# Gate products stacked into one fp32r product, and norm rows from two, in a decoder trunk

## The chip, the cores and the metric

One Trainium2 chip (trn2), of which the kernel uses one core. The metric is the device time of the kernel in microseconds. The kernel before ran three times: 2303.4, 2303.47 and 2307.49 us, median 2303.47. Profiles show one further execution of each kernel.

The engines are called as in the profile: PE (TensorE, matmuls; PEld is its weight load), DVE (VectorE), ACT (ScalarE), POOL (GpSimd) and SP (SyncE, which issues nearly all transfers).

## What is computed

A decoder trunk on 256 tokens of width 2048, two layers, in float32. Layer 0 mixes by gated linear attention (GLA, 4 heads), layer 1 by forgetting attention (FoX, 12 heads); each layer also attends to 256 memory tokens and ends in a gated MLP with a causal convolution of width 3. Cut to what the change touches:

```python
def rmsnorm(x, g):
    y = x * rsqrt(mean(x * x, axis=-1) + EPS)
    return y * g

# GLA: z = h @ w_in is split into q, k, v, glr, og, mq; glr is 16 wide
g = log_sigmoid(glr @ w_gate_up + b_gate) / 16        # forget gates, 4 heads x 256
o = gla_chunked(q, k, v, g)                           # 4 heads, o is 384 wide in each
o = o * rsqrt(mean(o * o, axis=-1) + EPS) * gn_gain   # a norm of each head's output
```

## The kernel before

The activations stay on the chip, features on the 128 partitions and the 256 tokens along the free dimension. The weights are streamed once, in units of up to 128x1024 floats: SP loads `raw` (L190), ACT rounds it to fp32r as `whi` (L191), and DVE subtracts (`wlo` = raw - whi, L200). Activations are split in the same way, high half and low half side by side in one tile of 2 x 256 columns. A float32 product is made of three fp32r products, high by high, low by high and high by low.

- `proj_fm` gives features on partitions. For each block of 128 rows, `product` (L222 to L228) issues `whi` against both halves at once (512 columns, L225 or L228) and `wlo` against the high half (256 columns, L226). `whole` (L233, L235) adds the two halves of the result.
- `proj_tm` gives tokens on partitions, with three products of up to 512 columns (L262 to L264).

Everything small is done in plain fp32: transposes by an identity, attention scores, and the two things that this case is about.

**Gates.** The first value panel also gives the 16 columns of `glr`, scaled by the norm's column. `turned` (L268 to L282) copies them to a zeroed tile (`narrow`, L274), transposes it (L279), and L491 copies the result to `glr`, 16 features on partitions 0 to 15 and zeros below. For each head `gates` loads 128x256 of `w_gate_up`, zero below row 16 (L510, two buffers), and for each of two halves multiplies it with `glr` (L514: fp32, 128x128 weights, 256 columns). ACT (L517 to L519) and DVE (L521 to L523) make the running sums of the log gates from it. The sums feed `core`, a head's attention by levels: subtractions (L578), exponentials (L579) and products (L581) on DVE and ACT, many small fp32 matmuls on PE (L595), masked copies back (L607).

**Norm rows.** A norm has a column `y`, one number for each token on its partition, found by Newton steps on DVE (L324 to L327), and a row, the same numbers along the free dimension on every partition, by which results with features on partitions are multiplied. `Norm.row` makes it once for each norm: DVE multiplies the identity by `y` for each half of the tokens (`dg`, L346), PE multiplies a matrix of ones by that diagonal (L348: fp32, 256 columns), and ACT copies the sum to `row` (L351). There are nine rows: memory, layer 0 input, four GLA heads, the two MLPs, and one for FoX.

**What sets the order.** The program is written in the order of the layers, and a scheduler places each engine's instructions when the kernel is built; each engine then takes its own in that order and waits on semaphores. Weight units are asked for 300 places ahead (`tc.high_priority`), with four buffers for `raw` and three each for `whi` and `wlo`. A heavier or lighter instruction can therefore move others on all engines.

Of the kernel before, what the change touches and what calls it, by code (L numbers as in the profile page):

```python
# [12 lines left out]
F32 = mybir.dt.float32  # L13
F32R = mybir.dt.float32r
I32 = mybir.dt.int32
AF = mybir.ActivationFunctionType
ALU = mybir.AluOpType
PSUM = bass.MemoryType.PSUM

P = 128  # L20
T = 256
# [4 lines left out]
GLA_H, DK, DV = 4, 256, 384  # L26
FOX_H, HD = 12, 128
MEM_H = 4
RANK = 16
# [108 lines left out]
def _trunk(ctx: ExitStack, tc: tile.TileContext, xt, xtok, memt, wp, wgu, gns, gfin, cnv, par, msk, out):  # L138
    nc = tc.nc
    where, _ = _layout()  # L140
    V, S, TE = nc.vector, nc.scalar, nc.tensor

    const = ctx.enter_context(tc.tile_pool(name="const", bufs=1))
    wpool = ctx.enter_context(tc.tile_pool(name="wpool", bufs=4))
    sm = ctx.enter_context(tc.tile_pool(name="small", bufs=2))
# [9 lines left out]
    ident = mask[:, M_ID : M_ID + P]  # L155
    ones = mask[:, M_ONE : M_ONE + P]
# [3 lines left out]
    def gain(name, i):  # L160
        c = C_GAIN[name] + i
        return gains[:, c : c + 1]

    eps = const.tile([P, 1], F32, name="eps")
    nc.gpsimd.memset(eps, EPS)
# [11 lines left out]
    def work(tag, bufs=1):  # L177
        return pwork.tile([P, 512], F32, name="ps_" + tag, tag=tag, bufs=bufs)
# [86 lines left out]
                if u == len(units) - 1:  # L265
                    evac(b, a)

    def turned(pool, bank, width, col):  # L268

        t = pool.tile([P, T], F32, name="narrow", tag="tmp", bufs=5)  # L270
        nc.gpsimd.memset(t, 0.0)

        def take(b, a):
            S.activation(t[:, b * P : b * P + width], a, AF.Copy, scale=col[:, b : b + 1])  # L274

        def turn():
            for b in range(2):
                bs = slice(b * P, (b + 1) * P)
                TE.transpose(bank[:, bs], t[:, bs], ident)  # L279
            return bank[:, :T]  # L280

        return take, turn  # L282
# [11 lines left out]
    class Norm:  # L294
# [45 lines left out]
        def row(self):  # L340

            if self.r is None:
                y = self.col()
                dg = sm.tile([P, T], F32, name="dg", tag="sq", bufs=2)
                for b in range(2):
                    V.tensor_scalar(dg[:, b * P : (b + 1) * P], ident, y[:, b : b + 1], None, ALU.mult)  # L346
                pr = work("t")
                TE.matmul(pr[:, :T], ones, dg, start=True, stop=True)  # L348
                self.r = sm.tile([P, T], F32, name="row", tag="rowx" if self.tag == "x" else "row",
                                 bufs=2 if self.tag == "x" else 1)  # L350
                S.activation(self.r, pr[:, :T], AF.Copy)  # L351
            return self.r
# [51 lines left out]
    nx = StreamNorm()  # L404
    with tc.tile_pool(name="load", bufs=1) as lp:
        mt = [lp.tile([P, 4, T], F32, name=f"mt{i}") for i in range(4)]

        def take_mem(g, half):
            n = 2 if g == 0 else 4
            if n == 2 or half == 0:  # L410
                i = half * 2
                nc.sync.dma_start(mt[g][:, i : i + n, :], memt[g, :, i : i + n, :])
                for i in range(i, i + n):
                    split(bufA, 4 * g + i, mt[g][:, i, :], gain("mem", 4 * g + i))
# [41 lines left out]
        for i in range(KC):  # L456
            split(bufB, i, xf[i], gain("mix0", i))
# [12 lines left out]
    def gla(nx):  # L470
        h, mix = bufB, bufA
        with tc.tile_pool(name="gla", bufs=1) as gp:
# [3 lines left out]
                nc.gpsimd.memset(t, 0.0)  # L476
            on = {}

            glr = gp.tile([P, T], F32, name="glr")

            def values(hd):
                return gp.tile([P, 2, DV], F32, name="gv", tag="gv", bufs=2)

            v0 = values(0)
            take, turn = turned(gp, work("t"), RANK, nx.col())

            def first_values(b, a):
                S.activation(v0[:, b, :], a[:, :DV], AF.Copy, scale=nx.col()[:, b : b + 1])
# [17 lines left out]
            def gates(hd):  # L506

                bc = gp.tile([P, 2, T], F32, name="bc", tag="bc", bufs=2)
                wg = gp.tile([P, DK], F32, name="wg", tag="wg", bufs=2)
                nc.sync.dma_start(wg, wgu[hd])  # L510
                for c in range(2):
                    f = 2 * hd + c
                    ps = work("s", 2)
                    TE.matmul(ps[:, :T], wg[:, c * P : (c + 1) * P], glr, start=True, stop=True)  # L514
                    bias = part[:, C_BG + f : C_BG + f + 1]
                    e = gp.tile([P, T], F32, name="ge", tag="tmp", bufs=5)
                    S.activation(e, ps[:, :T], AF.Abs, bias=bias)  # L517
                    S.activation(e, e, AF.Exp, scale=-1.0)
                    S.activation(e, e, AF.Ln, bias=1.0)  # L519
                    mz = gp.tile([P, T], F32, name="gm", tag="tmp", bufs=5)  # L520
                    V.tensor_scalar(mz, ps[:, :T], bias, 0.0, ALU.add, ALU.min)  # L521
                    V.tensor_tensor(mz, mz, e, ALU.subtract)
                    V.tensor_tensor_scan(bc[:, c, :], scanmask, mz, 0.0, ALU.mult, ALU.add)  # L523
                return bc
# [111 lines left out]
            for hd in range(GLA_H):  # L636
                bc = gates(hd)
                q = gp.tile([P, 2, T], F32, name="gq", tag="gq", bufs=2)
                k = gp.tile([P, 2, T], F32, name="gk", tag="gk", bufs=2)
                v = values(hd) if hd else v0  # L640
                proj_fm(("gq", hd), h, lambda c, a: V.scalar_tensor_tensor(
                    q[:, c, :], whole(a), DK ** -0.5, nx.row(), ALU.mult, ALU.mult))
                proj_fm(("gk", hd), h, lambda c, a: V.tensor_tensor(k[:, c, :], whole(a), nx.row(), ALU.mult))
                if hd == GLA_H - 1:
                    for j in range(OG_EARLY):
                        take_og(j)
                if hd:
                    proj_tm(("gv", hd), h, lambda b, a: S.activation(
                        v[:, b, :], a, AF.Copy, scale=nx.col()[:, b : b + 1]))
                core(hd, q, k, v, bc)  # L650
# [4 lines left out]
    def fox(nx, vt):  # L655
        hk, hq, mix = bufB, bufA, bufB
        stash = vt.rearrange("p b (i t) -> p (b i) t", t=T)
        with (
# [5 lines left out]
            for j in range(6):  # L664
                proj_fm(("fk", j), hk, lambda c, a, j=j: V.tensor_tensor(kt[:, 2 * j + c, :], whole(a), nx.row(), ALU.mult))
                for i in range(2 * j, 2 * j + 2):
                    split(hq, i, stash[:, i, :], gain("mix1", i))
            cs = fp.tile([P, T], F32, name="fc")
            cc = fp.tile([P, 2, FOX_H], F32, name="fcc")
            take, turn = turned(fp, work("s", 2), FOX_H, nx.col())  # L670

            def forget():
# [120 lines left out]
    def preparing(name, dst, also=None):  # L793
# [18 lines left out]
        return n, then  # L812

    gla(nx)
    n, then = preparing("ffn0", bufB)
    add_out(("wo", 0), bufA, then)
# [18 lines left out]
    with tc.tile_pool(name="store", bufs=1) as op:  # L835
        gf = op.tile([P, D], F32, name="gf")
        nc.sync.dma_start(gf, gfin.to_broadcast([P, D]))
        y = op.tile([P, 2, 512], F32, name="y")
# [93 lines left out]
```

## Time and profile before

| | |
|---|---|
| median of three runs | 2303.47 us |
| the profiled execution, its own time | 2304.12 us |
| its span, first to last instruction | 2302.3 us |
| granted PE clock, mean | 0.999 |
| PE matmul, busy | 2284.6 us |
| DVE, busy | 1614.8 us |
| ACT, busy | 1253.2 us |
| L348 (nine rows), matmul records | 18, 5.3 us busy |
| L514 (eight gate products), matmul records | 16, 5.1 us busy |
| GLA heads | 115 to 392 us of the span |

How to read it: the span is one execution, so it stands beside its own time and not beside the median. A matmul's duration holds its passage through the array, of which the next one covers a part; what it costs in a stream is the distance from its start to the next start. An engine's busy time says little of what it costs the kernel if another engine is the one that everything waits for; that is seen in the chain of work that ended last and in what ended an engine's idle time.

### The profile page before, as it was taken

How to read it: one execution, taken by the hardware profiler on the slowest of the kernel's cores; microseconds unless marked ns; L12 is line 12 of the kernel's file. 1: busy time of each engine (PE TensorE's matmuls, PEld its weight loads, DVE VectorE, ACT ScalarE, POOL GpSimd, SP SyncE). 2: the span in 40 equal slices, each digit the busy share in tenths (PEclk: the TensorE clock that was granted, in tenths of full speed). 3: DMA queues.
4: the chain of work that ended last, by engine and by line, in shares of the span. 5: the costliest groups of instructions: out<-in, count | busy, mean ns of one | idle time of the engine just before them, and what ended most of it. 6: DMA issues, size and time to landing. Idle time of an engine off the chain costs nothing.

```text
span 2302.3 us, 33124 instructions
## 1 busy us (share of the span) xinstructions
PE 2284.6 (99%) x12384; PEld 1976.7 (86%) x12384; DVE 1614.8 (70%) x2635; ACT 1253.2 (54%) x1958; POOL 3.0 (0%) x19
## 2 busy tenths in 40 slices
PE   8999999999999999999999999999999999999998
PEld 7889988888888888888888998888888888888886
DVE  7568987577765777557767557657776577756775
ACT  6555565555553555445565455556554455534554
POOL 0000000000000000000000000000000000000000
PEclk9999999999999999999999999999999999999999
DMA  8655555555555555555555564555555655565554
GB/s 309 200 160 158 156 158 179 188 183 190 187 191 193 191 188 188 192 192 191 186 184 189 176 195 157 167 190 187 189 191 191 193 185 190 189 195 190 186 191 156
DMA packets 124745, 430.14 MB, mean 187 GB/s; under 512 B 14108, under 2 KB 18600, under 8 KB 124456
## 3 DMA queue, kind: packets, MB, share of 16 engines
q1 hardware_dynamic: 124296, 427.50, 57.6%
q8 instruction: 97, 1.59, 0.3%
q14 instruction: 64, 0.52, 0.1%
q10 hardware_dynamic: 288, 0.52, 0.1%
HBM read 425.86 MB, written 2.11 MB: 186 GB/s over the span
## 4 chain that ended last, share of the span: by engine, by line
PE 99%; DMA 0%; ACT 0%; DVE 0%; issue 0%; SPq 0%; DVEq 0%; ACTq 0%
PE acc L225 37%; PE acc L226 20%; PE acc L263 12%; PE acc L264 12%; PE acc L262 12%; PE acc L228 2%; PE ps_s L806 0%; PE ps_s L595 0%; PE ps_t L380 0%; PE ps_s L387 0%; PE ps_o L398 0%; DMA mt<-memt 0%; PE ps_s L720 0%; PE ps_o L614 0%; PE ps_o L736 0%; PE ps_s L514 0%
## 5 line engine op out<-in xcount | busy, mean ns | idle before, releaser
L200 DVE TENSOR_TENSOR wlo<-raw,whi 128x1024 fp32r<-128x1024 f32 (+4 forms) x809 | 972.5, 1203 | 543.8 <-ACT whi L191 531.1
L191 ACT ACTIVATE whi<-raw 128x1024 fp32r<-128x1024 f32 (+4 forms) x809 | 843.2, 1043 | 772.0 <-PE acc L264 370.2
L225 PE MATMUL acc<-B,whi 128*128 128x512 f32 x1980 | 684.1, 396 | 0.0
L225 PE MATMUL acc<-A,whi 128*128 128x512 f32 x1680 | 580.7, 397 | 7.2 <-ACT whi L191 7.2
L226 PE MATMUL acc<-B,wlo 128*128 128x256 f32 x2112 | 551.1, 281 | 0.0
L226 PE MATMUL acc<-A,wlo 128*128 128x256 f32 x1792 | 464.6, 281 | 0.5 <-DVE wlo L200 0.5
L225 PEld LDWEIGHTS acc<-B,whi 128*128 128x128 f32 x1980 | 360.9, 188 | 69.0
L226 PEld LDWEIGHTS acc<-B,wlo 128*128 128x128 f32 x2112 | 397.6, 188 | 21.7
L225 PEld LDWEIGHTS acc<-A,whi 128*128 128x128 f32 x1680 | 305.8, 188 | 63.9 <-ACT whi L191 7.6
L226 PEld LDWEIGHTS acc<-A,wlo 128*128 128x128 f32 x1792 | 338.1, 189 | 21.1 <-DVE wlo L200 1.4
L263 PE MATMUL acc<-wlo,B 128*128 128x512 f32 (+3 forms) x736 | 274.9, 374 | 1.3 <-DVE wlo L200 1.3
L264 PE MATMUL acc<-whi,B 128*128 128x512 f32 (+3 forms) x736 | 274.0, 373 | 0.0
L262 PE MATMUL acc<-whi,B 128*128 128x512 f32 (+3 forms) x736 | 247.6, 372 | 0.0
L263 PE MATMUL acc<-wlo,A 128*128 128x512 f32 x544 | 212.4, 390 | 0.0
L264 PE MATMUL acc<-whi,A 128*128 128x512 f32 x544 | 211.8, 389 | 0.0
L262 PE MATMUL acc<-whi,A 128*128 128x512 f32 x544 | 192.9, 391 | 0.0
L233 ACT ACTIVATE part<-acc 128x256 f32<-128x256 f32 x240 | 90.1, 376 | 163.1 <-PE acc L228 163.1
L263 PEld LDWEIGHTS acc<-wlo,B 128*128 128x128 f32 x736 | 138.2, 188 | 21.1 <-DVE wlo L200 1.7
L264 PEld LDWEIGHTS acc<-whi,B 128*128 128x128 f32 x736 | 138.3, 188 | 18.7
L262 PEld LDWEIGHTS acc<-whi,B 128*128 128x128 f32 x736 | 137.5, 188 | 18.7
L235 DVE TENSOR_TENSOR wholes<-acc,part 128x256 f32<-128x256 f32 x240 | 101.1, 421 | 66.3 <-ACT part L233 65.9
L264 PEld LDWEIGHTS acc<-whi,A 128*128 128x128 f32 x544 | 102.1, 188 | 21.2
(196 smaller groups left out, 1565.6 us busy)
## 6 DMA issues: line engine op xcount, KB each, us to landing
raw<-wp SPq DMA_DIRECT2D x743, 512.0 KB, 3.4
raw<-wp SPq DMA_DIRECT2D x32, 384.0 KB, 3.1
raw<-wp SPq DMA_DIRECT2D x24, 388.0 KB, 3.1
raw<-wp SPq DMA_DIRECT2D x8, 400.0 KB, 3.2
xf<-xt SPq DMA_DIRECT2D x16, 128.0 KB, 4.8
x<-xtok SPq DMA_DIRECT2D x4, 512.0 KB, 7.2
mt<-memt SPq DMA_DIRECT2D x3, 512.0 KB, 7.7
cb<-cdram SPq DMA_DIRECT2D x12, 128.0 KB, 3.4
```

The costliest lines, as they stand in the source:

```text
L191: casts.append(S.activation(hi[:, s], raw[:, s], AF.Copy))
L200: V.tensor_tensor(lo[:, s], raw[:, s], hi[:, s].bitcast(F32), ALU.subtract)
L225: TE.matmul(a, hi[:, s], both, start=done == 0, stop=False)
L226: TE.matmul(a[:, :T], lo[:, s], both[:, 0, :], start=False, stop=False)
L228: TE.matmul(a, hi[:, s], both, start=False, stop=True)
L233: S.activation(t, a[:, T:], AF.Copy)
L235: V.tensor_tensor(r, a[:, :T], t, ALU.add)
L262: TE.matmul(a, xk[:, 0, xs], hi[:, s], start=u == 0 and j == 0, stop=False)
L263: TE.matmul(a, xk[:, 0, xs], lo[:, s], start=False, stop=False)
L264: TE.matmul(a, xk[:, 1, xs], hi[:, s], start=False, stop=last)
```

## The change

Gates: the copies of `glr` are written three times, at rows 0, 32 and 64 of the transposed tile: the value rounded to fp32r twice, and the remainder. The weights lie at the same three places (in the host's array). They are cast to fp32r on ACT, and rows 32 to 63 are replaced by the remainder on DVE. One fp32r product of 128 rows then sums high by high, high by low and low by high. `raw` weights and `wg` have one buffer each.

Norm rows: the column is split into a rounded part and a remainder, each gets its diagonal (one instruction with both halves of the tokens), and two fp32r products with an fp32r matrix of ones sum them. That matrix is a new constant. The split of activations and weights into two halves, and all other fp32 products, stay as they are.

```diff
+    onesr = const.tile([P, P], F32R, name="onesr")
+    nc.gpsimd.memset(onesr.bitcast(F32), 1.0)
...
-    def turned(pool, bank, width, col):
+    def turned(pool, bank, width, col, parts=False):
...
         def take(b, a):
-            S.activation(t[:, b * P : b * P + width], a, AF.Copy, scale=col[:, b : b + 1])
+            o = [t[:, b * P + i : b * P + i + width] for i in (0, 32, 64)]
+            if not parts:
+                S.activation(o[0], a, AF.Copy, scale=col[:, b : b + 1])
+                return
+            for i in range(2):
+                S.activation(o[i].bitcast(F32R), a, AF.Copy, scale=col[:, b : b + 1])
+            V.scalar_tensor_tensor(o[2], a, col[:, b : b + 1], o[0], ALU.mult, ALU.subtract)
...
                 y = self.col()
-                dg = sm.tile([P, T], F32, name="dg", tag="sq", bufs=2)
-                for b in range(2):
-                    V.tensor_scalar(dg[:, b * P : (b + 1) * P], ident, y[:, b : b + 1], None, ALU.mult)
+                y2 = [sm.tile([P, 2, 1], F32R, name=f"y{i}", tag=f"y{i}") for i in range(2)]
+                V.tensor_copy(y2[0], y.unsqueeze(2))
+                V.tensor_tensor(y2[1], y.unsqueeze(2), y2[0].bitcast(F32), ALU.subtract)
                 pr = work("t")
-                TE.matmul(pr[:, :T], ones, dg, start=True, stop=True)
+                for i, yi in enumerate(y2):
+                    dg = sm.tile([P, 2, P], F32R, name="dg", tag="sq", bufs=2)
+                    V.tensor_tensor(dg, ident.unsqueeze(1).to_broadcast([P, 2, P]),
+                                    yi.bitcast(F32).to_broadcast([P, 2, P]), ALU.mult)
+                    TE.matmul(pr[:, :T], onesr, dg, start=i == 0, stop=i == 1)
...
-            glr = gp.tile([P, T], F32, name="glr")
+            glr = gp.tile([P, T], F32R, name="glr")
...
-            take, turn = turned(gp, work("t"), RANK, nx.col())
+            take, turn = turned(gp, work("t"), RANK, nx.col(), True)
...
-                wg = gp.tile([P, DK], F32, name="wg", tag="wg", bufs=2)
-                nc.sync.dma_start(wg, wgu[hd])
+                raw = gp.tile([P, DK], F32, name="wgraw", tag="wgraw")
+                nc.sync.dma_start(raw, wgu[hd])
+                wg = gp.tile([P, DK], F32R, name="wg", tag="wg")
+                S.activation(wg, raw, AF.Copy)
+                V.tensor_tensor(wg[32:64], raw[32:64], wg[32:64].bitcast(F32), ALU.subtract)
...
-    wgu[:RANK] = a["gla_w_gate_up"][0]
+    for i in (0, 32, 64):
+        wgu[i : i + RANK] = a["gla_w_gate_up"][0]
```

## The prediction

> **What bounds the kernel now.** I read the page first: the busy shares, the slices, the chain that ended last.
>
> ```profile
> span 2302.3 us, 33124 instructions
> ## 1 busy us (share of the span) xinstructions
> PE 2284.6 (99%) x12384; PEld 1976.7 (86%) x12384; DVE 1614.8 (70%) x2635; ACT 1253.2 (54%) x1958; POOL 3.0 (0%) x19
> ...
> DVE  7568987577765777557767557657776577756775
> ...
> PEclk9999999999999999999999999999999999999999
> ...
> PE 99%; DMA 0%; ACT 0%; DVE 0%; issue 0%; SPq 0%; DVEq 0%; ACTq 0%
> ```
>
> PE is busy for 2284.6 of 2302.3 us at full granted clock, and the chain is PE for 99%. So time is PE's work plus its few waits. The waits view of PE alone lists 7.2 us for L225 (the first loads, before 12.7 us), 1.3 us for L263 and 0.5 us for L226; nothing else. A nanosecond taken from any matmul is a nanosecond of span, while VectorE (DVE) and ScalarE (ACT) work is free as long as they stay ahead of PE. DVE is nearest to the bound in slices 4 and 5 (230 to 345 us, the GLA heads), with digits 9 and 8.
>
> A busy PE is modelled, so what a matmul costs has to be read from starts. The timeline of PE, around a norm row (L348) and around a gate product (L514), columns start, duration:
>
> ```profile
> 51.84 0.39 PE L262 MATMUL acc<-whi,A 128*128 128x512 f32 x1
> 52.07 0.59 PE L348 MATMUL ps_t<-dg,mask 128*128 128x256 f32 x2
> 52.31 0.58 PE L262 MATMUL acc<-whi,A 128*128 128x512 f32 x1
> 52.73 0.39 PE L263 MATMUL acc<-wlo,A 128*128 128x512 f32 x1
> ...
> 162.17 0.60 PE L514 MATMUL ps_s<-glr,wg 128*128 128x256 f32 x2
> 162.41 0.47 PE L226 MATMUL acc<-B,wlo 128*128 128x256 f32 x1
> 162.72 0.39 PE L225 MATMUL acc<-B,whi 128*128 128x512 f32 x1
> 162.95 0.28 PE L226 MATMUL acc<-B,wlo 128*128 128x256 f32 x1
> 163.07 0.39 PE L225 MATMUL acc<-B,whi 128*128 128x512 f32 x1
> ```
>
> One fp32 product leaves two records (x2). An fp32r product of 512 columns takes 0.23 us from start to start (51.84 to 52.07), one of 256 columns 0.12 (162.95 to 163.07). From L348's start to the matmul after its successor are 52.73 - 52.07 = 0.66 us; less the successor's 0.23, **an fp32 product of 256 columns costs 0.43 us**. The gate gives the same: 162.72 - 162.17 = 0.55, less 0.12. The other places of both lines give 0.426 to 0.438. Where two L226 follow each other the spacing is 0.112 to 0.119, median 0.117.
>
> **The change, part by part.**
>
> *Gates.* Eight fp32 products (4 heads x 2) become eight fp32r ones of the same 256 columns: 8 x (0.432 - 0.117) = **-2.52 us**. The nearest row is L226, same shape and type; its bounds give -2.46 to -2.61.
>
> *Norm rows.* Nine fp32 products (18 records of L348) become eighteen fp32r ones: 9 x (0.432 - 2 x 0.117) = **-1.78 us**, by the bounds -1.7 to -1.9. I count no more: the built program has 9 more PE instructions, and otherwise the same ones in another order.
>
> The Trainium skill, page "TensorE: Matmul & The Clock Gate", section "Back-to-back issue gap", puts the isolated gap at N/2.4 + 2.5 ns, an estimate of 109 ns for 256 columns; by it the sum would be 8 x 0.323 + 9 x 0.214 = 4.5 us instead of 4.3. The trace shows 0.112 at the least, so I keep the row.
>
> *DVE.* Each row replaces two multiplications by two wider ones and gains two tiny ones; each head gains a subtraction. The rows:
>
> ```profile
> L346 DVE TENSOR_SCALAR dg<-mask,ny 128x128 f32<-128x128 f32 x18 | 4.3, 282 | 0.2
> L378 DVE TENSOR_SCALAR p<-p,rc 128x256 f32<-128x256 f32 x16 | 5.5, 352 | 0.5
> L522 DVE TENSOR_TENSOR gm<-gm,ge 128x256 f32<-128x256 f32 x8 | 3.3, 416 | 0.0
> L324 DVE TENSOR_TENSOR nt<-ny 128x2 f32<-128x2 f32 x27 | 4.2, 157 | 0.5
> ```
>
> The new diagonal has no row; L378 (0.35) and L522 (0.42) bound it, and L522 is the same operation, so 0.42. A row costs 2 x 0.42 + 2 x 0.16 - 2 x 0.28 = +0.6 us, nine of them 5.4. The weight subtractions add 4 x 0.42 = 1.7 and the low gate part 2 x 0.3: 7.7 us in all. The skill's page "VectorE: DVE Perf Modes", section "The perf-mode tier table", speaks against this trade: fp32 tensor_scalar in SBUF runs at 2x, tensor_tensor at 1x. L378 against L522 agrees (0.35, 0.42).
>
> I cost this at nothing, for two reasons. DVE has 687 us of idle time, and it runs ahead of PE: the first row's diagonal ends at 47.38 (lines L346 and L348 taken singly) and its product starts at 52.07; seven of nine have 3.5 us or more, the others 2.9 and 1.35 (at 238 us). 0.6 us fits into each. Without that cover, the heads' share is at risk: 4 rows x 0.6, 3 subtractions, 0.6 for the low part, 4.3 us.
>
> *ACT, SP, POOL.* Four casts of 128x256 (L518: 0.41) and two more narrow copies (L274: 0.26) come to 2.2 us of ACT, idle for 46% of the span. The added wait is at the first cast: ACT stands until its wgu load lands (issued at 38.95, 3.8 us: 42.75), with the next weight casts queued behind it and PE behind those. There ACT idles 1.66 us before the cast at 43.88 anyway, so it hides. Casts of later heads wait for the gate weights' single buffer; in the built order each stands right behind the Abs of the head before, which already waited for that product. The wgu loads, now single-buffered, stay within a few places of SP's queue; the load before has long been read. The POOL memset of 128x128 (0.2 us or so, by L476: 0.42 for 384) is needed at 52 us. The last matmul ends 8.7 us before the end; that tail isn't touched.
>
> **Sum.** -2.52 - 1.78 = -4.30 us. The profiled execution took 2304.12 us (span 2302.3 and 1.8 around it), so 2299.8 by its own time; it lies 0.65 us above the median of the runs, 2303.47, from which the sum is 2299.2. I say **2299.5 us**, 0.17% under the median. What a measurement of this kernel can tell from no change is about 0.2%, 4.6 us; the sum stops 0.3 us short of that line.
>
> **The rivals.**
>
> *Faster by more than the line.* The one PE wait in mid-kernel, 1.34 us at 1315.9, ends a chain that has nothing to do with PE's pace: ACT's table load at L677 (1.28 us), then the forget sums through memory (cdram, cb), and DVE standing at L715 for cb while the next wlo waits behind it. If the new order or the earlier PE moves it apart, 2303.5 - 4.3 - 1.3 = 2297.9. Against it: in the built order DVE and SP stand there as before. Shorter spacing (0.112) alone gives 2299.0. But 0.3 us is little beside runs that lie 4 us apart (2303.4 to 2307.49), so part of the forecast's own chance falls beyond the line.
>
> *DVE's cover is gone in the heads.*
>
> ```profile
> core 0: us, PE busy (x) PEld busy (x) DVE busy (x) ACT busy (x) POOL busy (x), PEclk, DMA share, GB/s
> 230.00:320.00 90.00, 90.00 (x601) 80.24 (x601) 83.56 (x212) 52.75 (x92) 0.00 (x0) 1.00 0.49 151
> ```
>
> Only 6.4 us of 90 are idle, and 2 rows and 2 subtractions add 2.0. If none of that hides, PE waits 2 us there, at most 4.3 over all heads: 2301 to 2303.5, still no measurable change. For it: the thin 6.4. Against it: what is added fits, and PE idles 0.0 there now.
>
> *Loads bind.* An LDWEIGHTS record lasts 0.188 us. If the new products went at that pace, gates would save 8 x 0.244 and rows 9 x 0.056: 2301.0. Against it: every L226 has its own load and goes at 0.117.
>
> *Slower.* The built order moves several hundred PE instructions among the heads (115 to 392 us). PE takes them in order, so a level product (L595) placed before its operands are made stops everything behind it, the weight products included. One such wait costs up to the whole level's chain: three subtractions (0.32 + 0.42 + 0.55, L578), the exponential (0.85, L579), three products (as much again), 3.4 us. Of the 12 level groups, two so caught come to 6.8 - 4.3 = 2.5 over, still within the line; from the third on it is slower: 10.2 - 4.3 = 5.9 over, 2309.4. For it: the thin DVE. Against it: the order was moved consistently on all engines, and before, the same kind of placement left PE without a wait in the heads.
>
> *It doesn't do what it says:* if an fp32r product of 256 columns took the fp32 time here, rows would cost 9 x 0.43 more and gates save nothing: 2307.4. L226 speaks against it.
>
> **Chances.** The forecast has 0.78: 0.48 of it within 0.2% and 0.30 beyond, for the 0.3 us. The stall that goes has 0.08 (faster), DVE's cover 0.05 and the loads 0.02 (both within), the re-ordered heads 0.06 (slower), no effect 0.01 (within). Faster 0.38, same 0.56, slower 0.06. The range, 2297.0 to 2304.5, takes in both sides of the sum, the stall, the heads' 4.3 us and the scatter; it leaves out the slower case.
>
> **What would show it.** The new row and gate products should leave one record each, 18 and 8, spaced 0.11 to 0.12; the next matmul should start no 25 ns after a second record. PE's busy time should fall by about 4.3 us and its waits stay at 7.2, 1.3 and 0.5. New PE waits on DVE between 115 and 392 us would show the heads rivals; a spacing of 0.19 the loads. I am wrong if PE waits in the heads add up to more than 2 us, or if fp32r after fp32 costs an extra start.

## The result, and the profile after

The changed kernel takes 2300.12 us (median of 22 runs, 2299.24 to 2301.63), the kernel before on the same chip 2303.4 us (22 runs, 2302.47 to 2307.49). The ratio is 0.9985, with a 95% interval of 0.9979 to 0.9991: 3.3 us less, inside the 0.2% that was set as the line. The profiled execution of the changed kernel took 2300.22 us, with a span of 2298.4.

The page after, first line, busy shares, DVE's slices and the chain that ended last:

```profile
span 2298.4 us, 33138 instructions
...
PE 2282.0 (99%) x12376; PEld 1974.0 (86%) x12376; DVE 1619.1 (70%) x2659; ACT 1253.6 (55%) x1964; POOL 3.1 (0%) x20
...
DVE  7569987577765777557767557657776577756775
...
PE 99%; DMA 0%; ACT 0%; DVE 0%; issue 0%; SPq 0%; DVEq 0%; ACTq 0%
```

PE still is the chain. Its records fall by 8 (16 gate records become 8, 18 row records become 18 single ones) and its busy time by 2.6 us, DVE's rises by 4.3. The waits view of PE alone (us in total, times, longest), in the kernel before and then after:

```profile
PE acc L225 <- ACT whi L191: 7.2, 2, 5.8
PE acc L263 <- DVE wlo L200: 1.3, 1, 1.3
PE acc L226 <- DVE wlo L200: 0.5, 1, 0.5
```

```profile
PE acc L227 <- ACT whi L193: 6.4, 3, 5.6
PE acc L265 <- DVE wlo L202: 0.8, 1, 0.8
PE acc L228 <- DVE wlo L202: 0.5, 1, 0.5
```

These are the same three places in both (every line is 2 further down after): the first loads, the stall at 1313 us, and one small wait. No wait of PE on DVE or ACT has come up in the GLA heads, and DVE, though busier there, is not late. The windows view over the heads (columns: length, PE, PEld, DVE, ACT, POOL busy with records, granted clock, DMA share, GB/s):

```profile
230.00:320.00 90.00, 90.00 (x592) 80.38 (x591) 85.10 (x219) 54.35 (x96) 0.00 (x0) 1.00 0.47 153
```

DVE's idle time of 6.4 us in this window of before (shown with the prediction) has become 4.9. The new diagonal is seen in the view of its line (ns min/median/max):

```profile
L360 DVE TENSOR_TENSOR dg<-mask,y x18: 407/418/422, 49.2 to 1569.0; 128x256 fp32r<-128x256 f32 x18
```

It was costed at 0.42. The Trainium skill, page "VectorE: DVE Perf Modes", section "The perf-mode tier table", gives tensor_tensor in fp32 the lowest tier, 1x, where tensor_scalar has 2x. The trace agrees in the order, and the diagonal with its broadcast operands has the price of the plain tensor_tensor (L522 before, 0.416); at this size the two operations are 0.06 us apart (0.352 for L378 before), far less than twofold.

PE's timeline after, around a norm row (L362) and a gate product (L531), columns start, duration:

```profile
1572.48 0.40 PE L228 MATMUL acc<-A,wlo 128*128 128x256 f32 x2
1572.71 0.28 PE L362 MATMUL ps_t<-dg,onesr 128*128 128x256 f32 x1
1572.83 0.39 PE L227 MATMUL acc<-A,whi 128*128 128x512 f32 x1
1573.05 0.28 PE L362 MATMUL ps_t<-dg,onesr 128*128 128x256 f32 x1
1573.17 0.28 PE L228 MATMUL acc<-A,wlo 128*128 128x256 f32 x1
...
160.05 0.28 PE L228 MATMUL acc<-B,wlo 128*128 128x256 f32 x1
160.16 0.28 PE L531 MATMUL ps_s<-glr,wg 128*128 128x256 f32 x1
160.28 0.40 PE L227 MATMUL acc<-B,whi 128*128 128x512 f32 x1
```

The new products leave one record each and take 0.12 us from start to start (1572.71 to 1572.83, 1573.05 to 1573.17, 160.16 to 160.28), as an L228 of the same size does; 16 of the 18 row products have 0.112 to 0.119. The other two (0.32 and 0.22, at 242.7 and 243.3 us) lie in and behind a run of the heads' level products, of which more below. Four of the eight gate products stand behind fp32 products and take 0.20 to 0.22: they carry the start that the fp32r product behind the old gate carried (162.41 to 162.72 in the timeline of before, 0.31 where 0.12 is usual), so it is no new cost.

**Where the time went.** In two executions of the changed kernel (this one and that of experiment 1), PE's starts keep the same distance to within 3 ns from 43 to 1311 us and to within 34 ns from 1320 us on. What differs lies at two places: the first loads and the stall at 1313 us. So the two traces can be laid side by side at the last product of each weight unit. After minus before, us:

| stretch | after - before | sum of the prediction |
|---|---|---|
| first loads, to 43 us | +0.36 | 0 |
| row of memory, 43 to 115 us | -0.21 | -0.20 |
| 115 to 128 us | -0.08 | 0 |
| row of layer 0 (at 128.2 us), 128 to 157 us | -0.09 | -0.20 |
| gates of the first head, 157 to 171 us | -0.58 | -0.63 |
| the other gates and the heads' rows, 171 to 400 us | -2.62 | -2.68 |
| row of the first MLP, 492 to 506 us | -0.08 | -0.20 |
| row of FoX, 1206 to 1264 us | -0.15 | -0.20 |
| all else from 400 to 1311 us | -0.10 | 0 |
| the stall at 1313 us (1.34 to 0.83) | -0.49 | 0 |
| FoX heads, 1356 to 1552 us | +0.21 | 0 |
| row of the second MLP, 1552 to 1610 us | -0.09 | -0.20 |
| the end | +0.03 | 0 |

Together these are -3.9, the difference of the spans. The first loads stand between -0.05 and +2.22 us against the kernel before in the profiles of the versions below, the stall between 0.8 and 1.5 us, with no order to it: scatter. Without those two, the trace gives **-3.8 us** where the sum said -4.3. The gates of the first head came nearly as costed, the other gates and the heads' rows did so together, the five rows outside the heads gave 0.62 of 0.99, and the FoX heads gave 0.2 us back.

### The profile page after: what moved, and what is told of

It is laid out like the page before. It is cut to its first block, busy times and chain, and to the rows that moved or that the text cites. A ratio compares the mean times of both kernels' runs of the same rounds, so it can differ in the third digit from the quotient of the medians.

```text
span 2298.4 us, 33138 instructions
## 1 busy us (share of the span) xinstructions
PE 2282.0 (99%) x12376; PEld 1974.0 (86%) x12376; DVE 1619.1 (70%) x2659; ACT 1253.6 (55%) x1964; POOL 3.1 (0%) x20
## 3 DMA queue, kind: packets, MB, share of 16 engines
q8 instruction: 97, 1.59, 0.3%
## 4 chain that ended last, share of the span: by engine, by line
PE 99%; DMA 0%; ACT 0%; DVE 0%; issue 0%; SPq 0%; DVEq 0%; ACTq 0%
PE acc L227 37%; PE acc L228 20%; PE acc L265 12%; PE acc L266 12%; PE acc L264 12%; PE acc L230 2%; PE ps_s L823 0%; PE ps_s L612 0%; PE ps_t L394 0%; PE ps_s L401 0%; PE ps_o L412 0%; DMA mt<-memt 0%; PE ps_s L737 0%; PE ps_o L753 0%; PE ps_o L631 0%; DMA cb<-cdram 0%
## 5 line engine op out<-in xcount | busy, mean ns | idle before, releaser
L228 PE MATMUL acc<-B,wlo 128*128 128x256 f32 x2112 | 550.1, 281 | 0.0
L228 PE MATMUL acc<-A,wlo 128*128 128x256 f32 x1792 | 464.9, 281 | 0.5 <-DVE wlo L202 0.5
L228 PEld LDWEIGHTS acc<-B,wlo 128*128 128x128 f32 x2112 | 397.5, 188 | 21.9
L228 PEld LDWEIGHTS acc<-A,wlo 128*128 128x128 f32 x1792 | 338.6, 189 | 21.1 <-DVE wlo L202 1.4
```

The source lines that it names most:

```text
L228: TE.matmul(a[:, :T], lo[:, s], both[:, 0, :], start=False, stop=False)
```

## The experiments

"Measured" is the median, and the ratio is to the kernel before, run beside it on the same chip. Extra work in these kernels is redundant or its result is not used.

**1 to 3: the change again, and each half alone.** Gates alone keeps the old `Norm.row`; rows alone keeps the old gates.

```diff
 # gates alone: Norm.row as before
...
-                    TE.matmul(pr[:, :T], onesr, dg, start=i == 0, stop=i == 1)
+                TE.matmul(pr[:, :T], ones, dg, start=True, stop=True)
...
 # rows alone: turned and gates as before
-            take, turn = turned(gp, work("t"), RANK, nx.col(), True)
+            take, turn = turned(gp, work("t"), RANK, nx.col())
...
```

The whole change, expected:

> The changed kernel once more, on the chip of the other three, as their mark. Theory (PE's spacing alone decides): 4.3 us under the kernel before by the sum, 3.3 by the medians already seen; between the two. Rival (the heads' thinner DVE gives back 1 us): 3.3 with PE waits of about 1 us between 115 and 392 us.

Measured: 2300.92 us against 2304.34, ratio 0.9983 (0.9974 to 0.9992): -3.4, with no wait of PE in the heads.

Gates alone, expected:

> Only the gates' product is stacked; norm rows stay one fp32 product. Theory: 8 x 0.315 = 2.5 us under the kernel before. Rival (the stacking's casts and subtractions in the heads cost PE time): 1.5 us or less under it. The eight gate products should leave one record each, 0.117 us apart from the next, and the span should fall by 0.6 us at the first two gates (160 to 163 us).

Measured: 2302.35 us, ratio 0.9993 (0.9984 to 1.0002): -2.0. From 43 to 1311 us its trace stands 1.91 us ahead of the kernel before, where 2.52 was expected; that is more than the 1.5 us of the rival and less than the theory's 2.5.

Rows alone, expected:

> Only the norm rows become two fp32r products; gates stay fp32. Theory: 9 x 0.2 = 1.8 us under the kernel before. Rival (a row saves only what the traces show at the two MLP rows, 0.09): 0.8 us under it.

Measured: 2302.93 us, ratio 0.9993 (0.9984 to 1.0002): -1.4. Its trace: -1.59 from 43 to 1311 us, +0.2 in the FoX heads, -0.09 at the last row, together about -1.5, between the theory's 1.8 and the rival's 0.8. The halves add up (2.0 + 1.4 = 3.4), each falls short of its term by 0.4 to 0.5, and the intervals are too wide to say so by the times alone; the traces say it (0.6 for the gates, 0.3 for the rows).

**4: DVE's cover.** Each diagonal is written three times, 36 instructions more. At 0.42 each that would be 15.1 us; by the page DVE is busy for 10.4 us more, since three in a row take 1.09 us.

```diff
+                    for _ in range(3):
-                    V.tensor_tensor(dg, ident.unsqueeze(1).to_broadcast([P, 2, P]),
+                        V.tensor_tensor(dg, ident.unsqueeze(1).to_broadcast([P, 2, P]),
...
```

> The changed kernel with each diagonal written three times over (same values): 36 more DVE instructions of 0.42 us, 15.1 us of DVE in all, 1.7 at each row and 6.7 us in the heads. Theory (DVE is covered): the time of the changed kernel within 0.5 us. Rival (no cover is left in the heads): up to 6.7 us more, with PE waits on DVE near 238, 283, 324 and 392 us.

Measured: 2300.93 us, ratio 0.9986 (0.9977 to 0.9995), the time of the whole change to 0.01 us. That they agree so well is partly luck: between 43 and 1311 us its trace loses 0.43 us against the changed kernel, and this is 0.75 lost from 171 to 400 us and 0.32 gained at rows outside the heads. The five rows outside gave 0.99 us here (0.39, 0.09, 0.13, 0.23 and 0.15 in order) where they gave 0.62. Their products are the same, but the build put the two of a row 6 to 10 weight products apart, where in the changed kernel they are 1 or 2 apart; at layer 0's row alone both stand at the same place in both versions, and that row gave the same 0.09. No new wait of PE shows. So over twice the DVE time that the change added (4.3 us by the page) does not use up the cover, and the rival in which the cover is gone falls. The 0.75 us in the heads come with another order of PE's products there; what made them was not traced further.

**5 and 6: the two prices by themselves.** Ten more fp32r products in each row of the changed kernel, five more fp32 products in each row of the kernel before.

```diff
 # in the changed kernel
+                    for _ in range(10 if i == 0 else 0):
+                        TE.matmul(pr[:, :T], onesr, dg, start=True, stop=True)
 # in the kernel before
+                for _ in range(6):
-                TE.matmul(pr[:, :T], ones, dg, start=True, stop=True)
+                    TE.matmul(pr[:, :T], ones, dg, start=True, stop=True)
```

fp32r, expected:

> The changed kernel with ten more fp32r products at each norm row (the same operands, overwritten by the real pair): 90 in all. Theory (0.117 us each, as the weight products of 256 columns): 10.5 us over the changed kernel. Rival (the weight load binds, 0.188 each): 16.9 over it.

Measured: 2310.39 us, ratio 1.0027 (1.0016 to 1.0039) to 2304.02 of the kernel before. The changed kernel there is 2304.02 - 3.4 = 2300.6, so 90 products cost 9.8 us, **0.109 us each**. In the timeline ten of them stand as one line:

```profile
1581.80 1.33 PE L363 MATMUL ps_t<-dg,onesr 128*128 128x256 f32 x10
1582.97 0.39 PE L364 MATMUL ps_t<-dg,onesr 128*128 128x256 f32 x2
```

The next product starts 1.17 us after the first of the ten: 0.117 each, and 0.113 to 0.120 over all such pairs of this trace. The weight loads, whose records last 0.188 us, would have made it 1.9; that rival falls. The median's 0.109 has an interval of about 0.03 to either side (the ratio's bounds over 90 products), so it doesn't choose between 0.117 and the estimate of 109 ns from the formula in the Trainium skill (page "TensorE: Matmul & The Clock Gate", section "Back-to-back issue gap"). The spacings in the trace do: none of the 81 is below 0.113, for weights that do not change. Over the whole trace, without the first loads and the stall, the 90 products add 9.9 us, 0.110 each: in places, what stands behind them runs faster than in the changed kernel, which the part on the rows below takes up.

fp32, expected:

> The kernel before with five more fp32 products at each norm row (overwritten by the real one): 45 in all. Theory (0.432 us each): 19.4 us over the kernel before. Rival (an fp32 product is cheaper than its neighbours' starts made it look, by the fifth that is missing from the sum, 0.35): 15.6 over it.

Measured: 2323.74 us, ratio 1.0085 (1.007 to 1.01): 19.7 us for 45 products, **0.438 us each**; in the trace two records that follow each other are 0.216 us apart, 0.431 a product. Both prices are the ones that the sum used (0.432 and 0.117), so what is missing in the sum is not in the products' own price.

**7 and 8: where a product lands.** The level products of the heads (L595 before) have weights of 64 columns, as some products ahead of them have, and stand in runs. In the traces a norm row falls into such a run in some versions, since the build moves the order. In gates alone, a run of 16 at 242 us is cut into 12 and 4; the two parts cost 0.95 and 0.62 us in place of 1.01. To price a cut, one fp32r product of 256 columns is added to each of the 12 runs, in the middle or behind it.

```diff
                                           dd[:, 4 * c + 2 * b + g, :], start=c == 0, stop=c == 1)
+                        if b == 0:     # in the middle; b == 1: behind
+                            TE.matmul(ps[:, T:], h[0][:, 0, :P], h[0][:, 0, :], start=True, stop=True)
```

In the middle, expected:

> The changed kernel with one more fp32r product of 256 columns (0.117 us, its result unused) in the middle of each of the 12 runs of sixteen level records. It is to be set against the same product behind each run. Theory (each cut in a run of 64-column products costs PE about 0.4 us): 12 x 0.4 = 4.8 us over the kernel with the product behind. Rival (only the number of products counts): the same time.

Measured: 2307.64 us, ratio 1.0016 (1.0006 to 1.0025).

Behind, expected:

> The changed kernel with the same extra product behind each of the 12 runs of level records. Both theories: 12 x 0.117 = 1.4 us over the changed kernel, 2302 us or a little under.

Measured: 2302.77 us, ratio 0.9993 (0.9983 to 1.0002), 2.1 us over the changed kernel by the medians, where 1.4 was expected; its trace stands 1.4 us behind the changed kernel's from 43 to 1311 us. The same twelve products cost 4.87 us more in the middle: **0.41 us a cut**. The traces are 5.4 us apart from 43 to 1311 us. The build moved other products too, and the heads have 35 runs of 64-column products in the first version and 21 in the second, so by the traces it is 0.39 for each of 14. PE's timeline in the middle version, and then in the other, over the same products (L612 the level run, L616 the added product, columns start, duration):

```profile
203.32 0.34 PE L266 MATMUL acc<-whi,B 128*128 128x384 f32 x1
203.59 0.55 PE L612 MATMUL ps_s<-gdd,gk 128*64 128x96 f32 x8
204.07 0.38 PE L616 MATMUL ps_s<-B 128*128 128x256 f32 x1
204.38 0.55 PE L612 MATMUL ps_s<-gdd,gk 128*64 128x96 f32 x8
204.86 0.39 PE L531 MATMUL ps_s<-glr,wg 128*128 128x256 f32 x1
205.09 0.34 PE L264 MATMUL acc<-whi,B 128*128 128x384 f32 x1
```

```profile
200.69 0.34 PE L265 MATMUL acc<-wlo,B 128*128 128x384 f32 x1
200.96 0.88 PE L612 MATMUL ps_s<-gdd,gk 128*64 128x96 f32 x16
201.77 0.39 PE L616 MATMUL ps_s<-B 128*128 128x256 f32 x1
201.99 0.28 PE L531 MATMUL ps_s<-glr,wg 128*128 128x256 f32 x1
202.11 0.34 PE L266 MATMUL acc<-whi,B 128*128 128x384 f32 x1
```

From the weight product ahead to the one behind, with sixteen level records and two fp32r products between them, it is 1.77 us in the first (203.32 to 205.09) and 1.42 in the second (200.69 to 202.11). The halves of eight take 0.48 us each where sixteen take 0.81, and the product between them stands for 0.31 where the one behind the whole run has 0.22 and the gate behind that 0.12. Counted with what it adds to the products on both sides of it, a run of these 64-column products costs about 0.4 us plus 0.034 for each record (2 records 0.46, 16: 1.01, 40: 1.77), and a product that cuts a run makes it pay about 0.4 again. The sum of the prediction had no such term. In the changed kernel it is nearly even, 20 runs before and after: the cut that a row makes at 242.7 us is set off by a run less elsewhere, which is luck. In gates alone there are 21.

**9 to 12: the 0.2 us in the FoX heads.** Every version with the new rows had them, gates alone did not. First the constant alone, in the kernel before (it is written and not used).

```diff
+    onesr = const.tile([P, P], F32R, name="onesr")
+    nc.gpsimd.memset(onesr.bitcast(F32), 1.0)
```

> The kernel before with the new constant tile alone (128x128 fp32r, written once and never read), which moves the later tiles by 512 bytes in each partition. Theory (PE's products alone decide): no change, PE starts equal to the nanosecond but for the first loads and the stall near 1316 us. Rival (the products' spacing depends on where the tiles lie): the FoX heads (1369 to 1480 us) take 0.2 us longer, as they do in every run that has the constant and in none that has not.

Measured: 2304.33 us against 2304.19, ratio 1.0 (0.9991 to 1.001). Behind the first loads its trace is that of the kernel before to within 1 ns up to the stall, and from the stall to the end. The constant does nothing.

Then the two small tiles of the split column alone, and the diagonal in one instruction alone, both in the kernel before, with its fp32 product:

```diff
 # small tiles
+                y2 = [sm.tile([P, 2, 1], F32R, name=f"y{i}", tag=f"y{i}") for i in range(2)]
+                V.tensor_copy(y2[0], y.unsqueeze(2))
+                V.tensor_tensor(y2[1], y.unsqueeze(2), y2[0].bitcast(F32), ALU.subtract)
 # one diagonal
-                for b in range(2):
-                    V.tensor_scalar(dg[:, b * P : (b + 1) * P], ident, y[:, b : b + 1], None, ALU.mult)
+                V.tensor_tensor(dg, ident.unsqueeze(1).to_broadcast([P, 2, P]),
+                                y.unsqueeze(2).to_broadcast([P, 2, P]), ALU.mult)
```

Small tiles, expected:

> The kernel before, with the split of the norm column added (two DVE instructions for each row, two more small tiles) and not used. What is asked is the stretch of the FoX heads, 1369 to 1495 us, which is 0.2 us longer in every kernel with the new rows and the same to the ns in the kernel with the constant alone. Theory: the small tiles move what is allocated behind them, and that is the 0.2: +0.2 us here too. Rival: it comes from the diagonal or the products: 0.0 here. The time itself stays within 0.3 us from 43 to 1311 us by either.

Measured: one run, 2304.92 us beside 2305.43. In the trace the FoX heads are +0.21 us, as in the changed kernel. And the stretches behind the rows at 494 and 1575 us are 0.16 and 0.15 us longer, though the row's product is the old one. But it does not stand at its old place: the build put it one weight product later at both rows, of which more below.

One diagonal, expected:

> The kernel before, with each diagonal written by one DVE instruction for both halves of the tokens, in place of two; the fp32 product and everything else as before. Theory (small tiles): 0.0 us in the FoX heads, 1369 to 1495 us. Rival (diagonal): +0.2 us. If neither run shows it, the products themselves are left as the cause.

Measured: one run, 2304.28 us; the FoX heads 0.00, the row at 1575 us 0.00, where the row also kept its place. So the FoX heads' 0.2 us come with the small tiles, not with the diagonal or the products. Last, the changed kernel with the small tiles padded, in the same order of instructions:

```diff
-                y2 = [sm.tile([P, 2, 1], F32R, name=f"y{i}", tag=f"y{i}") for i in range(2)]
+                y2 = [sm.tile([P, 2, 16], F32R, name=f"y{i}", tag=f"y{i}")[:, :, :1] for i in range(2)]
```

> The changed kernel with the two small tiles of a split column padded from 2 to 32 floats (two buffers each), so that they take 512 bytes of a partition in place of 32; order and instructions are the same. In the kernel with only the small tiles added, the FoX heads got 0.2 us longer and the stretches behind the rows at 494 and 1575 us 0.15 us each. Theory: the 32 bytes put what is allocated behind them at places where PE's 512-column products run about 2 ns longer, and 512 bytes do not. Then the rows at 494 and 1575 us save 0.2 us each (before minus this; the changed kernel 0.07 and 0.095), the FoX heads, 1369 to 1495 us, cost 0.0 (the changed kernel 0.2), and the trace stands 0.4 us or so ahead of the changed kernel's behind its first loads; ratio to the kernel before 0.998, which by the time alone can not be told from the changed kernel's 0.9985. Rival: it is the two added instructions, or any move of the tiles: 0.07, 0.095 and 0.2 as in the changed kernel.

Measured: 2300.61 us against 2304.48, ratio 0.9981 (0.9972 to 0.999): -3.9. The theory holds for the FoX heads and not for the rows. In the trace the FoX heads stand at 0.00 (the changed kernel +0.21), with the same two instructions, so the 0.2 us is a matter of places: of the small tiles themselves or of what is allocated behind them, which this run does not tell apart. The rows at 494 and 1575 us saved 0.07 and 0.09, as in the changed kernel: there the rival is right in that the other places of the tiles change nothing. PE's order is the same here as in the changed kernel, so the run can't tell the two instructions from the order in which the build set PE's products. Without the first loads and the stall, this trace gives -4.0 us, the best of all versions; by the times it can't be told from the changed kernel.

## Why the prediction held, and where its sum was off

**PE is the bound, and only its spacing counts.** Right. The chain is PE before and after, 10 us more of DVE moved the median by nothing that can be measured, and 90 and 45 more products moved it by 0.109 and 0.438 us each.

**The price of an edit is the change of spacing, not of busy time.** Right: the prices found by repetition are the spacings. But the page's busy time was expected to fall by about 4.3 us, and fell by 2.6; the other 1.3 of the spans' difference is idle time of PE (17.7 before, 16.4 after), that of the stall and the first loads among it. The busy column did not measure the edit.

**The sign "fp32r after fp32 costs an extra start".** Four of the new gate products do pay one (0.20 to 0.22 in place of 0.12), but there the product behind the old gate paid it, so the sum did not miss it. In a run of level products it was missed: the row at 242.7 us pays 0.32 and 0.22.

**Gates, -2.52.** Right for the first head (-0.58 where 0.63 was costed), and in sum for the other three heads with their rows (-2.62 where 2.68 was), which the whole change can't split. Alone the gates brought 1.9. One more run of 64-column products, cut by a row, stands for about 0.4 of the missing 0.6; the other 0.2 was not traced. The prediction held one number for a product wherever it lands; that step failed by about 0.4 us a cut.

**Rows, -1.78.** The signs and the records are as expected. **This is the mis-sized term.** In the heads it came: with rows alone the trace gained 0.98 us from 157 to 400 us, where four rows were to give 0.79. The five rows outside were to give 0.99 us and gave 0.62. The new products outside the heads take their 0.12 each; what is slower are the products behind. Right behind the row at 128.2 us the changed kernel has gained 0.20 us, and by 140 us it has lost 0.18 of that again. PE's timeline in the kernel before, and then in the one with the small tiles alone, behind the row at 494 us; left out are the 512-column products and twelve more of L226 between the two lines:

```profile
498.03 0.28 PE L226 MATMUL acc<-B,wlo 128*128 128x256 f32 x1
...
502.53 0.28 PE L226 MATMUL acc<-B,wlo 128*128 128x256 f32 x1
```

```profile
498.06 0.28 PE L226 MATMUL acc<-B,wlo 128*128 128x256 f32 x1
...
502.65 0.28 PE L226 MATMUL acc<-B,wlo 128*128 128x256 f32 x1
```

Thirteen pairs of products take 4.50 us in the first (0.346 a pair) and 4.59 in the second (0.353). From 494.5 to 508 us, 23 of 39 spacings behind a 512-column product are 0.230 in the kernel before and none is with the small tiles, where 20 of 37 lie between 0.236 and 0.241 and the spacings repeat in threes (0.241, 0.236, 0.233); in the changed kernel 7 of 38 are 0.230. Ahead of this stretch and behind it the mixture is much the same in all of them. So a row ahead sets the pace of some 40 products behind it, and before, the fp32 row happened to be followed by a fast stretch. For the old row, the pace goes by the place where the build puts it. PE's timeline around this row, in the kernel before and with the small tiles alone:

```profile
493.89 0.39 PE L225 MATMUL acc<-B,whi 128*128 128x512 f32 x1
494.12 0.59 PE L348 MATMUL ps_t<-dg,mask 128*128 128x256 f32 x2
494.37 0.47 PE L226 MATMUL acc<-B,wlo 128*128 128x256 f32 x1
```

```profile
494.45 0.28 PE L226 MATMUL acc<-B,wlo 128*128 128x256 f32 x1
494.57 0.59 PE L351 MATMUL ps_t<-dg,mask 128*128 128x256 f32 x2
494.81 0.58 PE L225 MATMUL acc<-B,whi 128*128 128x512 f32 x1
```

The old row stood behind a 512-column product; with the small tiles it stands one product later, behind a 256-column one, and the same holds at 1575 us. In the version with the one diagonal the old row stands two products later at 494 us, behind a 512-column product again, and at its old place at 1575 us: 0.00 at both. The changed kernel, its second execution, rows alone, both versions with the added products and the padded one have their rows at the same places at 494, 1229 and 1573 us, and there they gave the same to 0.01 us or so; with the tripled diagonals the places differ, and so do the gains. So what two tiny DVE instructions did here, they did by the built order. The place is not all: with ten more fp32r products the stretch behind the row at 1582 us is at 0.230 again, though these stand behind a 256-column product. No run changes a row's place and nothing else, and why it sets the pace stays open; no wait of PE shows. The loss behind layer 0's row is not covered by this: its place is the same in all versions.

**What was not in the sum:** the FoX heads' +0.21, a matter of where tiles lie, as the padded version shows. The sum's -4.30 less 0.37 for the rows outside and 0.21 here is -3.7; the trace has -3.8.

**DVE's 7.7 us at nothing.** Right in size too: taken singly, the instructions added less those that went come to 7.5 us; the page's busy time rose by 4.3, since it counts overlapping instructions once. Three diagonals in place of one cost a net 0.43 us of the trace, again without a wait.

**The rivals.** The stall did not go in any version (0.8 to 1.5 us); where it was shorter, no version shows an order in it. The DVE and load rivals fell by experiments 4 and 5. In the re-ordered heads no level product was caught waiting for its operands; what the order is seen to cost there is cuts. "Doesn't do what it says" falls by the single records.

**The forecast.** 2299.5 us was said and 2300.1 measured; -4.30 was summed, -3.8 is in the trace without its scatter, and -3.3 to -3.4 in the medians. The last 0.4 to 0.5 lie within the scatter of the first loads and the stall, and within the intervals. That the sum overshot was luck for the choice between the two sides of the line: a sum 0.3 us short of the line was nearer to it than the error of the sum.

## What to carry to other kernels

Where PE is the whole chain, price an edit by the spacing from start to start in its own stream; in fp32, a product of 256 columns is worth almost four of fp32r. Count then where the build places the edited products: here one that lands in a run of narrower ones pays for the run's start a second time, about 0.4 us, more than an fp32r product's own price. And don't expect a sum of tenths of a us to hold to its last tenth: the products behind a row ran here, with the place of the row, about 2% slower or faster for some 8 us without a single wait.

## What the runs showed of the hardware

- A run of fp32 products with weights of 64 columns, among fp32r products of 128, has a fixed cost of about 0.4 us for runs of 2 to 40 records (0.41 for a cut by the medians of the two versions, 0.39 by their traces); each record in it costs 0.034.
- From 494.5 to 508 us, where 512-column and 256-column fp32r products take turns, the spacing behind a 512-column product is 0.224 to 0.241 us, and one pace or another (all at 0.230, or in turns of 0.241, 0.236 and 0.233) is kept for about 8 us. The granted clock was 1.00 in both. Which it was went, for the fp32 row of the kernel before, with whether it stood behind a 512-column or a 256-column product.
- Where two small tiles took 32 bytes of each partition, 120 us of products much later were 0.21 us longer; where they took 512 bytes they were not. Which tiles were moved into which places was not looked at.
- PE's starts repeat between executions to 3 ns from 43 to 1311 us and to 34 ns behind the stall, where a transfer through memory ends (two executions of the changed kernel). So differences of 0.1 us can be read from single traces that the medians can't tell apart.
